# Two later places on a DMA queue: an encoder's attention bias tables, and the turning of an FFN's last gated half

## The chip, the cores and the metric

The kernel runs on one core of a Trainium2 chip. The metric is the device time of one execution in microseconds; lower is better. A program of this kind is one instruction stream per engine (TensorE, VectorE, ScalarE, GpSimd and SyncE), and the engines meet only at semaphores. In the profile they are PE (with PEld for its weight loads), DVE, ACT, POOL and SP. "SPq" and "POOLq" are the queues in which SyncE and GpSimd issue DMA transfers.

## The reference

The model is an encoder trunk with two layers over 512 tokens of width 1024, all in float32. What matters of it:

```python
def swiglu(x, w_in, w_out):
    g, u = jnp.split(x @ w_in, 2, axis=-1)          # 1024 -> 2 x 2816
    return (jax.nn.silu(g) * u) @ w_out             # 2816 -> 1024

def mixer(h, w_in, gate_bias, rpb, w_na_out, w_f_out, w_o):
    z = h @ w_in                                    # q, k, v, uf, ga, gf
    ...
    y_na = neighbourhood_attention(q, k, v, rpb) @ w_na_out
    y_f = fourier_mix(uf) @ w_f_out
    g_na = jax.nn.sigmoid(ga + gate_bias[0])
    g_f = jax.nn.sigmoid(gf + gate_bias[1])
    return (g_na * y_na + g_f * y_f) @ w_o

for l in range(2):
    x = x + 0.5 * swiglu(rms_norm(x, ffn1_norm[l]), ffn1_w_in[l], ffn1_w_out[l])
    x = x + mixer(rms_norm(x, mix_norm[l]), ...)
    x = x + 0.5 * swiglu(rms_norm(x, ffn2_norm[l]), ffn2_w_in[l], ffn2_w_out[l])
out = rms_norm(x, final_norm)
```

The attention adds a learned bias per head (from `rpb`) to its scores before the softmax. There are eight heads, and the kernel reads the bias as one expanded table of 384 KB per head.

## The kernel before

**Numbers.** Every float32 operand is split into a high and a low part, and each product is three matmuls (high x high, low x high, high x low; lines 508, 509 and 511). A granule of weights, 128 x 1024, is loaded by DMA into a buffer `raw`, ScalarE copies its high part (`whi`, three buffers), and VectorE subtracts to get the low part (`wlo`). The class `Stream` does this in a fixed order of granules: it loads 8 granules ahead (`FETCH`) and prepares 2 ahead (`AHEAD`) of the one that TensorE uses. Some granules are sums of two matrices. For these a second, accumulating load comes from POOL's queue, or VectorE adds two buffers (L164).

**Strassen.** Most products are one step of a Strassen-like scheme with seven products for a 2 x 2 block. Hence the names A, B, C, the product numbers 1 to 7, and the sums and differences of operands on VectorE.

**An FFN** (`stage_ffn`, four times) has an input half and an output half. The input half runs over blocks `jb` of 512 hidden features. Each block ends with two gated halves, one for each half of the tokens: `z2` (tokens 256 to 511, j = 1) after product 3, and `z1` (j = 0) after product 4. Each must be turned, so that features lie on partitions: `apart` copies the 16-bit words apart on ScalarE (`zs`, two copies, L346), SP issues a DMA transpose (`zt`, L347), and later `joined` copies the words together on ScalarE into a tile `at` (L356). The helper `halves` does the first two and puts the result on the list `turned`; `joined` takes the next from that list.

The output half is a list of 21 steps (product, chunk of rows): steps 0 to 2 are product 1, 3 to 5 product 2, then products 5, 6, 7, 3 for each of three chunks (6 to 17), and 18 to 20 product 4. `make(i)` forms the high and low part of step i's operand (names `c1h`, `c1l`, `c2h` and so on, after the product) up to two steps ahead. The last block's `z1` is read first by step 5, and its `z2` by the sum for step 15. Their joins are placed in the step loop:

```python
            if i == 3:
                turned.reverse()
                joined()
            if i == 5:
                joined()
```

**The mixer** (`stage_mixer`, twice) starts with products of the projection (`proj_UV`), with single projections of q and k between them. Its weight buffers come from a shared pool of slots. The bias tables (`bm`, four buffers) lie in the mixer's own pool, which is opened in the last steps of the FFN ahead, over the space of that FFN's weight buffers. `bias_for(hp)` loads the tables of two heads on SP's queue, and `Probs.maxes` (L1297) is their first reader.

**Order.** A scheduler orders each engine's instructions from the program's order and its own estimates of time. It may move an instruction ahead of others on its engine, DMA issues on SP included. `tc.keep_in_program_order(ins)` pins one instruction to its place, `tc.issue_after(ins)` puts what its block issues on the engine of `ins` behind `ins`, and `manual_schedule` keeps whole engines in program order for a block.

Of the kernel before, what the change touches and what calls it, by code (L numbers as in the profile page):

```python
# [13 lines left out]
U16 = mybir.dt.uint16  # L14
AF = mybir.ActivationFunctionType
# [3 lines left out]
P = 128  # L19
# [8 lines left out]
NH, DH = 8, 64  # L28
# [62 lines left out]
def encoder_kernel(  # L91
    ctx: ExitStack, tc: tile.TileContext, xin, xtr, wst, gains, gfin, gbias, bias_in, dft, chan, ident_in, rot, out
):
    nc = tc.nc
# [16 lines left out]
    def slot(dt=F32, s="k", shape=(4, 256)):  # L111
        return kp.tile([P, *shape], dt, tag="k", name=nm(s), bufs=23)
# [39 lines left out]
    class Item:  # L152
# [26 lines left out]
        def prep(self, nxt):  # L179
            n = self.raw.n  # L180
            hi = wp.tile([P, 1024], F32R, tag="whi", name=nm("whi"), bufs=3)[:, 0:n]
            lo = wp.tile([P, 1024], F32R, tag="wlo", name=nm("wlo"), bufs=3)[:, 0:n]
            t = self.raw.t
            self.summed()
            if self.neg:
                S.activation(hi, t, AF.Copy, scale=-1.0)  # L186
                self.last = V.scalar_tensor_tensor(lo, t, -1.0, hi.bitcast(F32), ALU.mult, ALU.subtract)  # L187
            else:
                for c in range(0, n, n // self.parts):
                    cs = slice(c, c + n // self.parts)  # L190
                    S.activation(hi[:, cs], t[:, cs], AF.Copy)  # L191
                    if nxt:
                        nxt.summed()
                    self.last = V.tensor_tensor(lo[:, cs], t[:, cs], hi[:, cs].bitcast(F32), ALU.subtract)  # L194
            if self.then:
                G.dma_start(out=t, in_=wst[GRAN_AT[self.then]][:, 0:n], accum_op=ALU.add)
            self.out = (hi, lo)
# [113 lines left out]
    ws = Stream()  # L311
# [26 lines left out]
            V.scalar_tensor_tensor(r, t, 1.5, r, ALU.add, ALU.mult)  # L338
        return r

    def apart(z):

        s, t = slot(U16, "zs", (2, 4, 2, P)), slot(U16, "zt", (2, 4, 256))
        words = z.bitcast(U16).rearrange("p b (q f h) -> p h q b f", q=4, h=2)
        for h in range(2):
            S.activation(s[:, h], words[:, h], AF.Copy)  # L346
        nc.sync.dma_start_transpose(  # L347
            out=t.rearrange("p h q (b t) -> p (h q b) t", b=2), in_=s.rearrange("p h q b f -> p (h q b f)")
        )
        return t  # L350

    def joined_words(to, t):

# [261 lines left out]
    def stage_ffn(norm, nxt, late):  # L615
# [75 lines left out]
        late_at, turned = [], []  # L691

        def halves(z, j, f0):

            turned.append((apart(z), j, f0))
# [26 lines left out]
        def settle_at():  # L722
            while late_at:
                to_at(*late_at.pop(0))
# [47 lines left out]
        def make(i):  # L772
            if i < len(steps) and i not in made:
                m, c, f = steps[i]
                made[i] = hl(f(), c, f"c{m}")
# [95 lines left out]
        for jb in range(0 if first else 1, NB):  # L871
            f0 = 2 + 4 * jb
            if first and jb == 0:
                with tc.manual_schedule(engines={mybir.EngineType.DVE, mybir.EngineType.Activation}):
                    pa = pair("A")
                    product(pa, acts[1], K4, True)
                    for j in range(2):
                        t = snap(pcl[j])
                        pcl[j] = [t[:, 0, :], t[:, 1, :]]
                    s1 = snap(pa)  # L880
                    second(s1)
                    pb = pair("B")
                    product(pb, acts[5], K4, True)
                    sb = snap(pb)
                    norm.rstd()
            else:
                pa, pb, s1, sb = two(jb)
                settle_at()
            product(pa, acts[6], K4, False, again=True)
            s2 = snap(pa)  # L890
            settle_at()
            if turned:
                joined()
            if jb or not first:
                second(s1)
            else:
                plain_out()
            z1 = gate(s1, 0)
            product(pa, acts[7], K4, False, again=True)
            if turned:  # L900
                joined()
            less(pa, sb)
            product(pb, acts[3], K4, False, again=True)
            less(pb, s2)
            if jb == NB - 1:
                make(0)
                make(1)
            z2 = gate(s2, 1)
            times(z2, [sb[:, 0, :], sb[:, 1, :]], 1)
            halves(z2, 1, f0)  # L910
            if jb == NB - 1:
                make(2)
            product(pa, acts[4], K4, False, again=True)
            times(z1, pa, 0)
            halves(z1, 0, f0)
# [4 lines left out]
        for i, (m, c, _) in enumerate(steps):  # L920
# [13 lines left out]
            )  # L934
            if i == 0:
                settle_at()
            if i == 3:
                turned.reverse()
                joined()
            if i == 5:  # L940
                joined()
            if m == 4 and c == 0 and not late:
                with tc.manual_schedule(engines={mybir.EngineType.DVE, mybir.EngineType.Activation}):
# [101 lines left out]
    def stage_mixer(l, norm, nxt):  # L1045
# [75 lines left out]
        def proj_UV():  # L1121

            acts, combine = combos(norm, None)
            ws.depth = 8
            steps = {m: combine(m) for m in (5, 6, 7, 4)}

            def step(m, n=1):
                for _ in range(n):
                    next(steps[m])

            step(5)
            def t1():
                step(5, 2)
                norm.squares(1, 0)

            pa = pair("A")
            product(pa, acts[1], K4, True, hook=t1)
            root = norm.rstd_steps()
            next(root)
            ws.items[ws.prepped + 1].summed()  # L1140
            next(root)
            norm.spread(R)
            ws.prep(ws.pos + 3)
            low10 = norm.quad_high(*norm.due.pop(0))
            s1 = snap(pa)
            norm.low01()
            step(6, 2)
            pb = pair("B")
            product(pb, acts[5], K4, True, hook=low10)
            sb = snap(pb)  # L1150
            S.activation(small("sq", 1), ones, AF.Exp)
            step(6)
            q0 = proj_T(DH**-0.5)
            step(7)
            product(pa, acts[6], K4, False, again=True, hook=lambda: step(7))
            s2 = snap(pa)
            k0 = proj_T(None)
            step(7)
            step(4, 2)
            q0 = q0()  # L1160
            step(4)
            pc = pair("C")
            product(pc, acts[2], K4, True)
            q[0] = q0()
            q1 = proj_T(DH**-0.5)
            k0 = k0()
            less(pc, s1)
            k[0] = k0()
            product(pb, acts[3], K4, False, again=True)
            q1 = q1()  # L1170
            less(pb, s2)
            uh, ul = slot(F32R, "uh", (2, T)), slot(F32R, "ul", (2, T))
            S.activation(uh, s2, AF.Copy)
            q[1] = q1()
            norm.flip()
            V.tensor_tensor(ul, s2, uh.bitcast(F32), ALU.subtract)
            S.activation(mir, mirror, AF.Copy)
            flipped = []

            def turn():  # L1180
                for c in range(2):
                    pm = bank()
                    PE.matmul(pm, mir, uh[:, 1 - c, :], start=True, stop=False)
                    PE.matmul(pm, mir, ul[:, 1 - c, :], start=False, stop=True)
                    t = tmp(s="uf")
                    S.activation(t, pm, AF.Copy, scale=norm.rflip[:, c : c + 1])
                    flipped.append(t)


            k1 = proj_T(None, hook=turn)  # L1190
            constants()
            us, ue = [[], []], []
            for c in range(2):
                for op in (ALU.add, ALU.subtract):
                    w = tmp(s="ue")
                    V.scalar_tensor_tensor(w, s1[:, c, :], norm.r[:, c : c + 1], flipped[c], ALU.mult, op)
                    ue.append(high_of(w, "u"))
                    us[c].append(None)
            for i, low_of in enumerate(ue):
                us[i // 2][i % 2] = low_of()  # L1200
            product(pa, acts[7], K4, False, again=True, ahead=0)
            ws.depth = FETCH
            return us, k1, pa, sb, acts[4]
# [55 lines left out]

        o, q, k, bms = [], {}, {}, {}  # L1260

        def bias_for(hp):
            bms[hp] = []
            for e in range(2):
                res = mp.tile([P, 3, 256], F32, tag="bm", name=nm("bm"), bufs=4)
                nc.sync.dma_start(out=res, in_=bias_in[(l * NH + 2 * hp + e)])
                bms[hp].append(res)

        def att_scores(i):
# [227 lines left out]
        with tc.manual_schedule(engines={mybir.EngineType.DVE, mybir.EngineType.Activation}):  # L1497
            with tc.manual_schedule(engines={mybir.EngineType.PE}):
                u, k1, pa, sb, acts4 = proj_UV()
                fp = [four_pos(0), four_pos(1)]  # L1500
                bias_for(0)
                k1 = k1()
                ws.prep(ws.pos + 2)
                bt = [rotated(fp[0])]
# [485 lines left out]
```

## Time and profile before

| | us |
|---|---|
| median of 3 runs | 1855.29 (1852.73 to 1857.38) |
| profiled execution | 1856.45 |
| its span, first to last instruction | 1854.7 |
| PE busy | 1841.4 (99%) |
| DVE busy | 1605.3 (87%) |
| ACT busy | 1311.6 (71%) |
| POOL busy | 171.5 (9%) |

The profile is of one execution. Its rows give a start, a duration and, in brackets, the idle time of that engine just before and what ended it. Matmuls overlap in TensorE, and their ends are modelled, so their pace is read from start to start. In a table of waits a row has the waiting engine, what released it, the time in total, the number of times and the longest. A row with "xN" stands for N instructions in a row. For a DMA issue the duration is that of the issue, not of the transfer.

### The profile page before, as it was taken

The numbers are of one execution on the slowest core, as the hardware profiler recorded it, in microseconds if no ns is written. First come the engines' busy times: TensorE is split into PE (matmuls) and PEld (weight loads), VectorE is DVE, ScalarE is ACT, GpSimd is POOL, SyncE is SP. The second block draws the span as 40 slices with busy tenths as digits, with TensorE's granted clock in tenths as the row PEclk, the third lists the DMA queues.
The fourth block names the chain that finished last, engine by engine and source line by source line (L and its number), as shares of the span: only waits on it lengthen the run. The fifth ranks groups of instructions, "written<-read, shape, count | busy, mean of one in ns | idle before, by whom it ended". The sixth has DMA issues, their size and how long they took to land.

```text
span 1854.7 us, 24607 instructions
## 1 busy us (share of the span) xinstructions
PE 1841.4 (99%) x8862; PEld 1530.4 (83%) x8862; DVE 1605.3 (87%) x1950; ACT 1311.6 (71%) x1780; POOL 171.5 (9%) x210
## 2 busy tenths in 40 slices
PE   9999999999999999999999999999999999999997
PEld 7888888888888888888788888888888888888886
DVE  7878899786989987889998888997869899887898
ACT  6777875668676777777666777766676776777865
POOL 0001010100111100001010100101001101000010
PEclk9999999999999999999999999999999999999999
DMA  9898798933886788879888887988249867889794
GB/s 302 227 231 218 197 272 271 226 97 105 251 230 174 183 219 226 210 201 269 243 197 222 225 219 196 271 281 205 70 154 235 226 174 182 233 206 217 220 285 133
DMA packets 198458, 394.21 MB, mean 213 GB/s; under 512 B 103808, under 2 KB 103936, under 8 KB 198336
## 3 DMA queue, kind: packets, MB, share of 16 engines
q1 hardware_dynamic: 169664, 294.30, 49.3%
q0 software_dynamic: 28528, 98.33, 29.6%
q8 instruction: 69, 1.13, 0.3%
q14 instruction: 53, 0.43, 0.1%
q10 hardware_dynamic: 144, 0.02, 0.0%
HBM read 365.85 MB, written 2.11 MB: 198 GB/s over the span
## 4 chain that ended last, share of the span: by engine, by line
PE 92%; DVE 4%; DMA 2%; issue 1%; ACT 1%; SPq 0%; DVEq 0%; POOL 0%; ACTq 0%; POOLq 0%
PE A L508 10%; PE A L511 10%; PE A L509 10%; PE o L511 6%; PE o L508 6%; PE o L509 6%; PE B L509 5%; PE B L508 5%; PE B L511 5%; PE ps L315 4%; PE ps L316 3%; PE ps L317 3%; PE C L508 3%; PE C L509 3%; PE C L511 3%
## 5 line engine op out<-in xcount | busy, mean ns | idle before, releaser
L194 DVE TENSOR_TENSOR wlo<-raw,whi 128x1024 fp32r<-128x1024 f32 (+1 forms) x534 | 631.5, 1192 | 172.0 <-ACT whi L191 171.3
L191 ACT ACTIVATE whi<-raw 128x1024 fp32r<-128x1024 f32 (+1 forms) x534 | 546.0, 1033 | 255.9 <-DVE raw L164 61.2
L150 POOL DMA_DIRECT2D raw<-in_wst_dram x166 | 144.3, 891 | 1341.8 <-DMA raw<-in_wst_dram 754.2
L164 DVE TENSOR_TENSOR raw<-raw,raw 128x1024 f32<-128x1024 f32 (+1 forms) x150 | 178.8, 1193 | 2.0
L509 PE MATMUL A<-whi,xl 128*128 128x512 f32 x400 | 155.7, 389 | 0.0
L508 PE MATMUL A<-whi,xh 128*128 128x512 f32 x400 | 155.7, 389 | 0.0
L356 ACT ACTIVATE at<-zt 128x1024 uint16<-128x1024 uint16 (+2 forms) x96 | 110.4, 1168 | 19.0 <-DMA zt<-zs 19.0
L186 ACT ACTIVATE whi<-raw 128x1024 fp32r<-128x1024 f32 (+1 forms) x83 | 86.0, 1036 | 47.0 <-issue 12.5
L511 PE MATMUL A<-wlo,xh 128*128 128x512 f32 x400 | 115.0, 389 | 0.0
L187 DVE SCALAR_TENSOR_TENSOR wlo<-raw,whi 128x1024 fp32r<-128x1024 f32 (+1 forms) x83 | 98.4, 1194 | 11.3 <-ACT whi L186 11.3
L511 PEld LDWEIGHTS A<-wlo,xh 128*128 128x128 f32 x400 | 75.1, 188 | 15.6
L508 PEld LDWEIGHTS A<-whi,xh 128*128 128x128 f32 x400 | 75.1, 188 | 15.4
L509 PEld LDWEIGHTS A<-whi,xl 128*128 128x128 f32 x400 | 75.1, 188 | 15.4
L508 PE MATMUL C<-whi,xh 128*128 128x512 f32 x208 | 81.1, 390 | 0.3 <-ACT whi L191 0.3
L509 PE MATMUL C<-whi,xl 128*128 128x512 f32 x208 | 81.0, 389 | 0.0
L509 PE MATMUL B<-whi,xl 128*128 128x512 f32 x208 | 81.0, 389 | 0.0
L508 PE MATMUL B<-whi,xh 128*128 128x512 f32 x208 | 80.9, 389 | 0.0
L346 ACT ACTIVATE zs<-th 128x1024 uint16<-128x1024 uint16 x80 | 79.4, 1041 | 0.9 <-DVE th L737 0.9
L730 ACT ACTIVATE th<-sn,rh 128x512 f32<-128x512 f32 x80 | 55.1, 716 | 34.0 <-DVE sn L583 33.1
L578 ACT ACTIVATE sn<-A 128x512 f32<-128x512 f32 x104 | 59.0, 584 | 24.8 <-PE A L511 24.8
L511 PE MATMUL C<-wlo,xh 128*128 128x512 f32 x208 | 59.8, 389 | 0.0
L511 PE MATMUL B<-wlo,xh 128*128 128x512 f32 x208 | 59.8, 389 | 0.0
(438 smaller groups left out, 4680.2 us busy)
## 6 DMA issues: line engine op xcount, KB each, us to landing
raw<-in_wst_dram SPq DMA_DIRECT2D x470, 512.0 KB, 5.8
raw<-in_wst_dram POOLq DMA_DIRECT2D x174, 512.0 KB, 7.9
raw<-in_wst_dram SPq DMA_DIRECT2D x30, 256.0 KB, 4.2
bm<-in_bias_dram SPq DMA_DIRECT2D x16, 384.0 KB, 3.6
x<-in_xin_dram SPq DMA_DIRECT2D x4, 512.0 KB, 10.2
raw<-in_wst_dram POOLq DMA_DIRECT2D x8, 256.0 KB, 9.3
dft<-in_dft_dram POOLq DMA_DIRECT2D x8, 256.0 KB, 4.3
gb<-in_gbias_dram SPq DMA_DIRECT2D x4, 512.0 KB, 15.1
```

Source lines behind the costliest of these rows:

```text
L150: G.dma_start(out=self.t, in_=wst[GRAN_AT[self.plus]][:, 0 : self.n], accum_op=ALU.add)
L164: V.tensor_tensor(self.raw.t, self.raw.t, self.add.t, ALU.add)
L186: S.activation(hi, t, AF.Copy, scale=-1.0)
L187: self.last = V.scalar_tensor_tensor(lo, t, -1.0, hi.bitcast(F32), ALU.mult, ALU.subtract)
L191: S.activation(hi[:, cs], t[:, cs], AF.Copy)
L194: self.last = V.tensor_tensor(lo[:, cs], t[:, cs], hi[:, cs].bitcast(F32), ALU.subtract)
L315: PE.matmul(ps, lh, rh, start=start, stop=False, skip_group_check=again)
L346: S.activation(s[:, h], words[:, h], AF.Copy)
L356: S.activation(to[:, w], t[:, w], AF.Copy)
L508: PE.matmul(ps, lh, rh, start=start, stop=False, skip_group_check=again)
L509: PE.matmul(ps, ll, rh, start=False, stop=False, skip_group_check=again)
L511: PE.matmul(ps, lh, rl, start=False, stop=stop, skip_group_check=again)
```

## The change

It has two parts.

In the mixer, the first call of `bias_for` moves from behind the projection (where `four_pos` has run) to an earlier place in the program, after the third product of the projection, and its two loads are pinned to that place in SP's order.

In an FFN's last block, `z2` is still copied apart where it was, but its DMA transpose is issued only after step 1 of the output half, pinned to that place. So `z1`, turned at the end of the block, is on the list first. The join of `z1` stays at step 3 and is placed on ScalarE behind the high part of the last weights that have been prepared; the join of `z2` moves from step 5 to step 7. To this end `apart` is divided into `words_apart` and `turned_words`, and the weights' preparation keeps its ScalarE instruction as `first`.

```diff
@@ Item.prep
-                S.activation(hi, t, AF.Copy, scale=-1.0)
+                self.first = S.activation(hi, t, AF.Copy, scale=-1.0)
...
-                    S.activation(hi[:, cs], t[:, cs], AF.Copy)
+                    self.first = S.activation(hi[:, cs], t[:, cs], AF.Copy)
@@
-    def apart(z):
-
-        s, t = slot(U16, "zs", (2, 4, 2, P)), slot(U16, "zt", (2, 4, 256))
+    def words_apart(z):
+
+        s = slot(U16, "zs", (2, 4, 2, P))
         words = z.bitcast(U16).rearrange("p b (q f h) -> p h q b f", q=4, h=2)
         for h in range(2):
             S.activation(s[:, h], words[:, h], AF.Copy)
-        nc.sync.dma_start_transpose(
+        return s
+
+    def turned_words(s):
+
+        t = slot(U16, "zt", (2, 4, 256))
+        return t, nc.sync.dma_start_transpose(
             out=t.rearrange("p h q (b t) -> p (h q b) t", b=2), in_=s.rearrange("p h q b f -> p (h q b f)")
         )
-        return t
+
+    def apart(z):
+
+        return turned_words(words_apart(z))[0]
@@ stage_ffn, the last block
-            halves(z2, 1, f0)
             if jb == NB - 1:
+                z2 = words_apart(z2)
                 make(2)
+            else:
+                halves(z2, 1, f0)
@@ stage_ffn, the steps of the output half
+            if i == 1:
+                t, ins = turned_words(z2)
+                tc.keep_in_program_order(ins)
+                turned.append((t, 1, f0))
             if i == 3:
-                turned.reverse()
-                joined()
-            if i == 5:
+                with tc.issue_after(ws.items[ws.prepped - 1].first.ins):
+                    joined()
+            if i == 7:
                 joined()
@@ stage_mixer, proj_UV
             s2 = snap(pa)
+            bias_for(0, True)
             k0 = proj_T(None)
@@
-        def bias_for(hp):
+        def bias_for(hp, pinned=False):
             bms[hp] = []
             for e in range(2):
                 res = mp.tile([P, 3, 256], F32, tag="bm", name=nm("bm"), bufs=4)
-                nc.sync.dma_start(out=res, in_=bias_in[(l * NH + 2 * hp + e)])
+                ins = nc.sync.dma_start(out=res, in_=bias_in[(l * NH + 2 * hp + e)])
+                if pinned:
+                    tc.keep_in_program_order(ins)
                 bms[hp].append(res)
@@
                 fp = [four_pos(0), four_pos(1)]
-                bias_for(0)
                 k1 = k1()
```

## The prediction, made before the changed kernel was run

> **What bounds the kernel now.** I read the head of the page first, then the table of what TensorE waited for, then its matmuls in order of time.
>
> ```profile
> span 1854.7 us, 24607 instructions
> PE 1841.4 (99%) x8862; PEld 1530.4 (83%) x8862; DVE 1605.3 (87%) x1950; ACT 1311.6 (71%) x1780; POOL 171.5 (9%) x210
> ...
> PE o L511 <- DVE wlo L194: 1.3, 2, 0.7
> PE ps L136 <- DVE ones L132: 1.2, 1, 1.2
> PE C L508 <- ACT whi L191: 0.3, 1, 0.3
> PE cl L509 <- DVE xl L325: 0.3, 1, 0.3
> PE wC L509 <- DVE m2l L322: 0.2, 1, 0.2
> ...
> 235.36 0.39 PE L508 MATMUL o<-whi,c2h 128*128 128x512 f32 x1
> ...
> 244.88 0.39 PE L508 MATMUL o<-whi,c2h 128*128 128x512 f32 x1
> 245.11 0.39 PE L509 MATMUL o<-whi,c2l 128*128 128x512 f32 x1
> ```
>
> The reader is to see an engine that almost never stops: all waits that the table lists add to 3.3 us. Between 235.36 and 244.88 lie two steps of the output half of an FFN (a first chunk with three row tiles, 18 matmuls, and a second with four, 24): 9.52 us / 42 = 0.2267 us from start to start, though one matmul is shown as 0.39. Small delays hide in that overlap, so I compare equal stretches instead. The output half of an FFN, step loop from its first to its last matmul, runs four times (start and end, length, then busy time and count of PE, PEld, DVE, ACT, POOL, granted clock, DMA share, GB/s):
>
> ```profile
> 220.40:327.86 107.46, 107.46 (x487) 89.22 (x486) 104.32 (x108) 76.72 (x97) 12.63 (x15) 1.00 0.94 263
> 818.36:928.60 110.24, 109.50 (x487) 88.47 (x486) 106.39 (x110) 77.24 (x98) 12.96 (x15) 1.00 0.89 249
> 1140.16:1248.40 108.24, 108.13 (x488) 88.95 (x487) 104.23 (x108) 76.89 (x97) 12.53 (x15) 1.00 0.93 262
> 1739.20:1844.92 105.72, 105.06 (x463) 86.45 (x461) 103.18 (x118) 70.73 (x84) 10.41 (x12) 1.00 0.77 216
> ...
> 315.21 1.91 PE L413 MATMUL tr<-ident,x 128*128 128x128 f32 x16
> ```
>
> The first three have 462 matmuls and 24 transposes; the last has no transposes. Sixteen transposes last 1.91 us with the end of the last one, so 24 are worth some 2.6 us, and the last stretch compares with 107.46 - 2.6 = 104.86. Against the best of them (the first) the others lose 2.78, 0.78 and 0.86 us: 4.4 us in all. That is the whole stock from which the FFN part of the change can gain, 0.24% of the time. The second thing to see is VectorE: 104.32 of 107.46 us busy, 97%. In this stage it has 3 us of slack, so an idle microsecond of VectorE early in it can come back as a stall of TensorE. I take 0.3% of the median, 5.6 us, as about what a measurement of this kernel can tell from no change.
>
> **The bias tables (twice, once a layer).** The change moves two 384 KB loads on SP's queue and nothing else: from an early place, chosen without a fixed order, to behind the weight loads that the program has issued by then.
>
> ```profile
> SPq L1266 <- DVE wlo L194: 13.6, 1, 13.6
> ...
> 321.81 0.80 SPq L1266 DMA_DIRECT2D bm<-in_bias_dram  x2
> 322.66 0.90 SPq L148 DMA_DIRECT2D raw<-in_wst_dram  x2
> 323.60 0.91 SPq L1266 DMA_DIRECT2D bm<-in_bias_dram  x2
> 324.61 3.77 SPq L148 DMA_DIRECT2D raw<-in_wst_dram  x4
> ...
> L1297 DVE CUSTOM_DVE_ANT_0 s<-ps,bm x64: 402/419/425, 395.7 to 1371.4; 128x256 f32<-128x256 f32 x64
> ...
> DMA to landing us min/median/max: 2.8/3.6/8.4
> ```
>
> SP's queue stands 13.6 us at the first table, until VectorE has left the old weight buffers, and six weight loads stand behind it. What that wait costs today is nothing: the table of TensorE's waits names no weights of the mixer's first products, so removing it gains 0. What the new place can cost: by my count the tables come after those six loads, so near 328.4 (324.61 + 3.77), and land by 328.4 + 8.4 = 336.8 at the slowest. Their first reader, the row maxima, starts at 395.7, 59 us later. So 0 on this side too. If the queue should stand still at one of those six loads for 59 us more, the first scores would wait; no row of the queue near there has such a wait. The second pair (323.60) isn't pinned. It can now be the one that comes first and waits the 13.6 us; then this part does nothing at all. ScalarE, POOL and VectorE see no instruction more or less. Value 0, ends -0.5 and +0.5 us (the size of the smaller waits in TensorE's table).
>
> **The FFN's last block (four times).** Nothing is added: four copies that split words and four that join them on ScalarE, and two DMA transposes on SP, stay. Three things move.
>
> First, the transpose of the second token half (j = 1) goes behind that of the first half, to after step 1. On SP's queue:
>
> ```profile
> 223.48 4.54 SPq L347 DMA_TRANSPOSE zt<-zs  x1
> 228.11 1.01 SPq L148 DMA_DIRECT2D raw<-in_wst_dram  x2
> 229.48 3.69 SPq L347 DMA_TRANSPOSE zt<-zs  x1
> 233.26 2.82 SPq L148 DMA_DIRECT2D raw<-in_wst_dram  x3
> ...
> raw<-in_wst_dram SPq DMA_DIRECT2D x470, 512.0 KB, 5.8
> raw<-in_wst_dram POOLq DMA_DIRECT2D x174, 512.0 KB, 7.9
> ```
>
> Two weight loads come up to 4.5 us earlier; those behind the new place come up to 4.5 us later. Loads are issued eight granules ahead, each worth 12 matmuls x 0.2267 = 2.72 us, so 21.8 us; a load and an accumulating load on top take 5.8 + 7.9 = 13.7. The 8.1 us between them cover a shift of 4.5. Without that cover it would cost up to 4.5 us a time. The first half's transpose keeps its place at 229.48: it waits for its own two copies on ScalarE, so it lands no earlier.
>
> Second, the join of the first half (2 copies, L356) is held on ScalarE behind the last prepared weights, which at that point are the second granule of step 4. Its row of before and the neighbours, in the first FFN and in the second:
>
> ```profile
> 235.11 1.06 ACT L191 ACTIVATE whi<-raw 128x1024 fp32r<-128x1024 f32 x1 [0.98 <-PE o L509]
> 236.08 2.57 ACT L356 ACTIVATE at<-zt 128x1024 uint16<-128x1024 uint16 x2
> 238.51 1.03 ACT L191 ACTIVATE whi<-raw 128x1024 fp32r<-128x1024 f32 x1
> 239.45 1.04 ACT L321 ACTIVATE c2h<-at 128x1024 fp32r<-128x1024 f32 x1
> ...
> 237.58 1.22 DVE L194 TENSOR_TENSOR wlo<-raw,whi 128x1024 fp32r<-128x1024 f32 x1
> 239.57 1.23 DVE L194 TENSOR_TENSOR wlo<-raw,whi 128x1024 fp32r<-128x1024 f32 x1 [0.78 <-ACT whi L191]
> 240.72 1.22 DVE L322 TENSOR_TENSOR c2l<-at,c2h 128x1024 fp32r<-128x1024 f32 x1
> ...
> 833.86 2.58 ACT L356 ACTIVATE at<-zt 128x1024 uint16<-128x1024 uint16 x2 [3.30 <-DMA zt<-zs]
> 836.31 1.03 ACT L191 ACTIVATE whi<-raw 128x1024 fp32r<-128x1024 f32 x1
> ...
> 837.38 1.23 DVE L194 TENSOR_TENSOR wlo<-raw,whi 128x1024 fp32r<-128x1024 f32 x1 [1.76 <-ACT whi L191]
> ...
> 1160.54 1.23 DVE L194 TENSOR_TENSOR wlo<-raw,whi 128x1024 fp32r<-128x1024 f32 x1 [1.99 <-ACT whi L191]
> ...
> 1758.38 1.22 DVE L194 TENSOR_TENSOR wlo<-raw,whi 128x1024 fp32r<-128x1024 f32 x1 [0.79 <-ACT whi L191]
> ```
>
> First FFN. The weights copy at 238.51 would now come first. It reuses the buffer (one of three) of step 3's first granule, whose last reader is the eighth matmul: 235.36 + 7 x 0.2267 + 0.39 = 237.3. So copy 237.3 to 238.4, join to 240.8, the operand's high part (c2h) to 241.8, its low part on VectorE to 243.0. TensorE needs it at 245.11: 2.1 us to spare, where before it had 245.11 - 240.72 - 1.22 = 3.2. No direct stall. Queued behind the held join on ScalarE are c2h and the weights of step 5, on VectorE the low parts that follow. VectorE: its wait of 0.78 goes, but after the second weights (ready at 238.4, done 237.58 + 1.14 x 2 = 239.9) it now waits for c2h until 241.8: 1.9 us instead of 0.78, so about 1.1 worse. The third FFN shows what that is worth: with 1.99 idle at the same place its stretch is 0.78 us longer than the first one's. I take +0.8 for the first FFN, and the same for the fourth (0.79 idle now). The third is already in that state: 0. In the second FFN the 3.30 us wait for the transpose goes, as the weights at 836.31 no longer stand behind it; but VectorE is no further at the end of this passage: now it does both weights' low parts and c2l from 837.38 on, three operations of 1.15 (239.57 to 240.72), to 840.8; by the working of the first FFN, which lies 818.36 - 220.40 = 597.96 earlier, c2l as the last of the three would end at 243.0 + 597.96 = 841.0. The gain is only in the earlier release of a weight buffer. That FFN loses 2.0 us more than the third with the same idle there; I take a third of it, -0.6.
>
> Third, the join of the second half goes from step 5 to step 7, 2.6 us of ScalarE's time. Its reader is the sum for step 15, far behind; ScalarE is 71% busy in this stretch (76.72 of 107.46). Taken at 0; without the cover, up to 2.6 us.
>
> **Sum.** 0.8 - 0.6 + 0 + 0.8 + 0 = +1.0 us. The profiled execution took 1856.45 us, of which its span is 1854.7 and 1.75 lie around it; it is 1.16 above the median of 1855.29. By the profile 1857.4; moved to the median, 1856.3. The bounds: -4.4 if all four stretches become as good as the best, and +6.7 (the slower rival).
>
> **The rivals.** *Slower: VectorE can't make it up.* The held join costs VectorE 1.9 us or more in each FFN, the late second join takes ScalarE from the weights at step 7, and accumulating loads then run late as in the second FFN. The price, if all four become as bad as the worst stretch shown: 2.78 + 0 + (2.78 - 0.78) + (2.78 - 0.86) = 6.7 us, 1862.0. Place: the weights' low parts in steps 7 to 17. It decides when VectorE's idle time in a stretch passes the 3 us of slack. For it: 97% busy. Against it: 1.1 us of new idle in two of four.
>
> *The waits go and all of the loss with them:* -4.4, 1850.9. For it: the 3.30 us row and the 1.76 behind it are just what the pin attacks. Against it: c2h itself moves behind the weights. It stays within 0.3%.
>
> *It doesn't do what it says:* the second pair of tables takes the first one's wait, and transposes and joins fall where other waits hide them: 1855.3.
>
> *TensorE's matmul time isn't the bound:* if weights loads set the pace and matmuls only stretched over waits that the change shortens, the four stretches could fall to their PEld time: 431.7 - 353.1 = 78.6 us less, 1776.7. Against it: 42 matmuls at an even 0.2267 us in a stretch where nothing is waited for. The Trainium skill, "Perfetto Trace Analysis", section "Identifying the Most-Contended Engine", says that matmul busy time is a poor measure of how near a kernel is to its limit and that LDWEIGHTS busy time should be taken. By that rule the 83% would leave much room; the even starts speak for a full engine.
>
> **How the numbers follow.** Forecast (a net of -2 to +3 us, no change that can be told) 0.50; no effect 0.15; all of the loss gone 0.15; the slower rival, from 5 us up, 0.17, of which 0.01 stays below 5.6 us; the matmul rival 0.01; 0.02 for a gain over 5.6 us from places that the profile doesn't show as waits. Faster by over 0.3%: 0.03. Slower by over 0.3%: 0.16. Within: 0.81. Predicted 1856.3. The range goes from 1850.9 to 1861.5, into the lower part of the slower case.
>
> **What would show it.** Right: the four stretches at about 108.3, 109.6, 108.2 and 106.5 us; no wait of L356 for its transpose in the output halves; a weights copy ahead of L356 in each; VectorE's wait before c2l near 2 us; the first bias load with no 13.6 us before it, or that wait passed on to the second pair. Wrong: a stretch over 111 us, TensorE waiting for c2l or for weights in steps 5 to 9, or a mixer whose first products wait.

## The result and the profile after

The changed kernel takes 1858.26 us (median of 16 runs, 1856.83 to 1862.26), the kernel before 1855.42 beside it (16 runs, 1852.73 to 1857.64). The ratio is 1.0014, 95% interval [1.0008, 1.0021]: slower by some 2.6 us. The interval doesn't hold 1, so the difference is real, but it is less than the 0.3% that I had named as the bound. The profiled execution took 1858.61 us, its span is 1856.8, 2.1 above the span of before.

The head of its page, and rows of the table of what TensorE waited for (total, times, longest). L511 and L509 of before are now L519 and L517:

```profile
span 1856.8 us, 24633 instructions
PE 1841.3 (99%) x8862; PEld 1529.3 (82%) x8862; DVE 1605.3 (86%) x1950; ACT 1310.7 (71%) x1780; POOL 171.0 (9%) x210
...
PE o L519 <- DVE wlo L194: 1.4, 2, 0.7
PE ps L136 <- DVE ones L132: 1.2, 1, 1.2
PE A L516 <- ACT sn L586: 0.7, 1, 0.7
PE cl L516 <- ACT whi L191: 0.6, 1, 0.6
PE ps L316 <- DVE xl L426: 0.4, 2, 0.2
```

All busy times are the same within 1.1 us. The last three of these rows are not in the table of before, nor are two more of 0.3 us. Rows for `A L516` and `cl L516` also stand in profiles of kernels without a loss (0.2 and 0.8 us in e7 below). `ps L316 <- DVE xl` comes twice, in the first projection of each mixer; of the fourteen profiles of this document just those eight have it whose mixers start late. The four output halves (start and end, length, busy times and counts, clock, DMA share, GB/s):

```profile
220.37:327.88 107.51, 107.51 (x487) 89.09 (x486) 104.03 (x108) 75.53 (x93) 12.48 (x15) 1.00 0.94 274
818.96:927.55 108.59, 107.93 (x487) 89.01 (x486) 105.37 (x109) 76.61 (x97) 12.80 (x15) 1.00 0.90 252
1139.13:1247.49 108.36, 108.29 (x488) 88.80 (x487) 104.05 (x108) 75.47 (x93) 12.60 (x15) 1.00 0.93 272
1739.91:1847.11 107.20, 106.11 (x463) 86.04 (x461) 103.19 (x118) 70.45 (x84) 10.35 (x12) 1.00 0.76 213
```

Against before they are +0.05, -1.65, +0.12 and +1.48 us: together nothing. So the loss isn't where the FFN part works, or the single profile hides it; the runs below look at both. On SP's queue the bias tables stand where they were expected, without a wait, and their first reader comes 68 us later:

```profile
300.28 28.13 SPq L148 DMA_DIRECT2D raw<-in_wst_dram  x15
328.46 0.90 SPq L1281 DMA_DIRECT2D bm<-in_bias_dram  x2
339.41 0.33 SPq L148 DMA_DIRECT2D raw<-in_wst_dram  x1
339.79 0.91 SPq L1281 DMA_DIRECT2D bm<-in_bias_dram  x2
...
L1314 DVE CUSTOM_DVE_ANT_0 s<-ps,bm x64: 400/418/425, 396.5 to 1371.2; 128x256 f32<-128x256 f32 x64
```

The held join in the first FFN, on ScalarE and VectorE in order of time (idle time before, and what ended it, in brackets):

```profile
237.42 1.07 ACT L191 ACTIVATE whi<-raw 128x1024 fp32r<-128x1024 f32 x1 [1.25 <-PE o L517]
238.39 2.57 ACT L364 ACTIVATE at<-zt 128x1024 uint16<-128x1024 uint16 x2
240.82 1.03 ACT L191 ACTIVATE whi<-raw 128x1024 fp32r<-128x1024 f32 x1
241.75 1.04 ACT L321 ACTIVATE c2h<-at 128x1024 fp32r<-128x1024 f32 x1
...
237.54 2.34 DVE L194 TENSOR_TENSOR wlo<-raw,whi 128x1024 fp32r<-128x1024 f32 x2
241.88 1.23 DVE L194 TENSOR_TENSOR wlo<-raw,whi 128x1024 fp32r<-128x1024 f32 x1 [2.00 <-ACT whi L191]
243.03 1.22 DVE L322 TENSOR_TENSOR c2l<-at,c2h 128x1024 fp32r<-128x1024 f32 x1
```

VectorE now idles 2.00 us there, as worked out (1.9), yet this stretch is within 0.05 us of before. On SP's queue the first half's transpose, which comes first now, has not kept its place:

```profile
226.94 1.86 SPq L352 DMA_TRANSPOSE zt<-zs  x1
228.89 1.03 SPq L148 DMA_DIRECT2D raw<-in_wst_dram  x1
229.97 4.04 SPq L352 DMA_TRANSPOSE zt<-zs  x1
```

It is issued at 226.94 instead of 229.48, because ScalarE's two copies for it start 2.5 us earlier (224.93 instead of 227.46), with fewer weights copies ahead of them.

### The profile page after: what moved, and what is told of

It is laid out like the page before. It is cut to its first block, busy times and chain, and to the rows that moved or that the text cites. A ratio compares the mean times of both kernels' runs of the same rounds, so it can differ in the third digit from the quotient of the medians.

```text
span 1856.8 us, 24633 instructions
## 1 busy us (share of the span) xinstructions
PE 1841.3 (99%) x8862; PEld 1529.3 (82%) x8862; DVE 1605.3 (86%) x1950; ACT 1310.7 (71%) x1780; POOL 171.0 (9%) x210
## 4 chain that ended last, share of the span: by engine, by line
PE 85%; DVE 6%; DMA 4%; issue 3%; ACT 2%; POOL 0%; SPq 0%; DVEq 0%; ACTq 0%; POOLq 0%
PE A L516 9%; PE A L517 9%; PE A L519 9%; PE o L519 5%; PE o L517 5%; PE o L516 5%; PE B L516 5%; PE B L517 5%; PE B L519 5%; PE ps L315 3%; PE ps L316 3%; PE ps L317 3%; DMA raw<-in_wst_dram 3%; PE C L517 2%; PE C L516 2%
## 5 line engine op out<-in xcount | busy, mean ns | idle before, releaser
L517 PE MATMUL A<-whi,xl 128*128 128x512 f32 x400 | 155.7, 389 | 0.0
L516 PE MATMUL A<-whi,xh 128*128 128x512 f32 x400 | 155.7, 389 | 0.0
L364 ACT ACTIVATE at<-zt 128x1024 uint16<-128x1024 uint16 (+2 forms) x96 | 111.0, 1168 | 12.5 <-DMA zt<-zs 12.5
L519 PE MATMUL A<-wlo,xh 128*128 128x512 f32 x400 | 115.1, 389 | 0.0
L519 PEld LDWEIGHTS A<-wlo,xh 128*128 128x128 f32 x400 | 75.1, 188 | 15.6
L517 PEld LDWEIGHTS A<-whi,xl 128*128 128x128 f32 x400 | 75.1, 188 | 15.5
L516 PEld LDWEIGHTS A<-whi,xh 128*128 128x128 f32 x400 | 75.1, 188 | 15.4
L517 PE MATMUL C<-whi,xl 128*128 128x512 f32 x208 | 81.0, 389 | 0.0
L517 PE MATMUL B<-whi,xl 128*128 128x512 f32 x208 | 81.0, 389 | 0.0
L516 PE MATMUL C<-whi,xh 128*128 128x512 f32 x208 | 80.9, 389 | 0.0
L516 PE MATMUL B<-whi,xh 128*128 128x512 f32 x208 | 80.9, 389 | 0.0
L519 PE MATMUL B<-wlo,xh 128*128 128x512 f32 x208 | 59.8, 389 | 0.0
L519 PE MATMUL C<-wlo,xh 128*128 128x512 f32 x208 | 59.8, 389 | 0.0
```

Source lines behind the costliest of these rows:

```text
L364: S.activation(to[:, w], t[:, w], AF.Copy)
L516: PE.matmul(ps, lh, rh, start=start, stop=False, skip_group_check=again)
L517: PE.matmul(ps, ll, rh, start=False, stop=False, skip_group_check=again)
L519: PE.matmul(ps, lh, rl, start=False, stop=stop, skip_group_check=again)
```

## Where the time went

I looked for the first place where the same matmul starts later than in the kernel before and stays late. It is the mixer's start. The matmuls of TensorE in the kernel before and then in the changed one, first those that end the first FFN, then the mixer's first projection, then the end of the mixer's product 6 (start, duration):

```profile
327.41 0.61 PE L511 MATMUL o<-wlo,c4h 128*128 128x512 f32 x2
339.65 0.39 PE L315 MATMUL ps<-xh,whi 128*128 128x512 f32 x1
339.88 0.39 PE L316 MATMUL ps<-xl,whi 128*128 128x512 f32 x1
350.08 0.62 PE L511 MATMUL A<-wlo,t6h 128*128 128x512 f32 x2
```

```profile
327.43 0.61 PE L519 MATMUL o<-wlo,c4h 128*128 128x512 f32 x2
339.67 0.39 PE L315 MATMUL ps<-xh,whi 128*128 128x512 f32 x1
340.29 0.50 PE L316 MATMUL ps<-xl,whi 128*128 128x512 f32 x1 [0.22 <-DVE xl L426]
350.85 0.61 PE L519 MATMUL A<-wlo,t6h 128*128 128x512 f32 x2
```

22.67 us before, 23.42 after: 0.75 us, though the table of waits owns up to 0.2. VectorE shows why. Before, then after:

```profile
287.47 1.22 DVE L750 TENSOR_TENSOR at<-at,at 128x1024 f32<-128x1024 f32 x1
...
315.42 1.22 DVE L322 TENSOR_TENSOR c4l<-at,c4h 128x1024 fp32r<-128x1024 f32 x1
...
325.66 1.23 DVE L187 SCALAR_TENSOR_TENSOR wlo<-raw,whi 128x1024 fp32r<-128x1024 f32 x1 [1.17 <-ACT whi L186]
326.81 1.22 DVE L418 TENSOR_TENSOR xl<-xr,xh 128x1024 fp32r<-128x1024 f32 x1
327.94 1.28 DVE L756 SCALAR_TENSOR_TENSOR x<-o,x 128x512 f32<-128x512 f32 x2
...
338.05 1.22 DVE L418 TENSOR_TENSOR xl<-xr,xh 128x1024 fp32r<-128x1024 f32 x1
```

```profile
313.12 2.47 DVE L764 SCALAR_TENSOR_TENSOR x<-o,x 128x512 f32<-128x512 f32 x4
315.52 1.21 DVE L758 TENSOR_TENSOR at<-at,at 128x1024 f32<-128x1024 f32 x1
...
318.92 1.21 DVE L322 TENSOR_TENSOR c4l<-at,c4h 128x1024 fp32r<-128x1024 f32 x1
...
326.74 0.68 DVE L764 SCALAR_TENSOR_TENSOR x<-o,x 128x512 f32<-128x512 f32 x1
328.09 0.69 DVE L764 SCALAR_TENSOR_TENSOR x<-o,x 128x512 f32<-128x512 f32 x1 [0.66 <-PE o L519]
328.69 1.22 DVE L426 TENSOR_TENSOR xl<-xr,xh 128x1024 fp32r<-128x1024 f32 x1
...
339.01 1.22 DVE L426 TENSOR_TENSOR xl<-xr,xh 128x1024 fp32r<-128x1024 f32 x1
```

The edit moved a join at step 3 and one at step 5. At step 20, some 70 us later, the scheduler has put the sum for the last operand (`at<-at`) behind four updates of x (315.52); before, the last sum of this half started at 287.47. The last `c4l` comes 3.5 us later, the work behind it shifts, and in the end the mixer's first `xl` stands behind two updates of x, the second of which waits for the FFN's last matmul. Before, it stood ahead of them: 328.69 instead of 326.81. At the next `xl` 0.96 us of that is left (339.01 against 338.05), and TensorE waits for it. Most of the delay is still there when the second output half begins: from the matmul at 327.64 to the first of that half it is 490.72 us before (818.36 - 327.64) and 491.30 after (818.96 - 327.66).

## The experiments

Each of these kernels ran in five rounds beside the kernel before. Diffs are against the changed kernel unless another is named. All but e2 have the bias tables in their new place. In the table "turned late" says whether the second half's transpose comes after step 1, "held" whether the first join is placed behind the last prepared weights, and "second join" gives its step; "start" is the time from the FFN's last matmul to a fixed later one in the first and in the second mixer (22.44 in the kernel before: from 327.64, the second of its row at 327.41, to 350.08); "second" and "last" are the lengths of the output halves, one profile each.

| kernel | turned late | held | second join | ratio to before, 95% | start | second | last |
|---|---|---|---|---|---|---|---|
| before | no | no | 5 | 1 | 22.44, 26.97 | 110.24 | 105.72 |
| e1 tables only | no | no | 5 | 0.9998 [0.9989, 1.0006] | 22.44, 26.97 | 109.53 | 105.15 |
| changed | yes | yes | 7 | 1.0014 [1.0008, 1.0021] | 23.19, 27.75 | 108.59 | 107.20 |
| e2 FFN part only | yes | yes | 7 | 1.0012 [1.0002, 1.0022] | 23.19, 27.77 | 109.06 | 106.81 |
| e3 | yes | yes | 5 | 1.0041 [1.0029, 1.0053] | 23.19, 27.73 | 108.56 | 109.30 |
| e4 | yes | no | 7 | 1.0005 [0.9997, 1.0014] | 23.19, 27.77 | 107.82 | 107.31 |
| e5 sum first | yes | yes | 7 | 1.0011 [1.0003, 1.0020] | 22.44, 26.97 | 108.42 | 107.45 |
| e6 | no | no | 7 | 1.0033 [1.0020, 1.0045] | 23.19, 27.73 | 109.22 | 108.66 |
| e7 | yes | no | 5 | 0.9992 [0.9983, 1.0001] | 22.44, 26.97 | 107.40 | 108.35 |
| e8 | no | yes | 7 | 1.0017 [1.0008, 1.0026] | 23.19, 27.72 | 109.19 | 106.35 |
| e9 | in the first three | no | 5 | 0.9988 [0.9979, 0.9997] | 22.44, 26.97 | 107.40 | 106.67 |
| e10 | first three: as changed | | | 1.0006 [0.9997, 1.0015] | 23.19, 27.76 | 108.82 | 104.87 |
| e11 | no | yes | 5 | 1.0013 [1.0004, 1.0022] | 23.19, 27.73 | 107.61 | 109.73 |
| e12 | in the last | no | 5 | 1.0002 [0.9993, 1.0011] | 22.44, 26.97 | 107.88 | 105.79 |

**Each part alone (e1, e2).** e1 is the kernel before with the `bias_for` lines of the change, e2 the change without them.

> Only the mixer's part of the change: the first bias tables pinned behind the weights, the FFNs as before. Theory A (all of the loss comes from the FFN part, through the order of ScalarE and VectorE; the tables are free): the time of before, 1855.4 us, within 1 us, with the 13.6 us wait of SP's queue gone or passed on and TensorE's start of the mixer at an unchanged distance from the end of the FFN. Theory B (the six weight loads that now start some 13 us earlier disturb the end of the FFN or the mixer's first products): +1.3 us or more, of which about 0.7 us shows in each layer in the 20 us after the mixer's first matmul.

> Only the FFN part of the change: the bias tables where they were. Theory A: the same loss as the whole change, 1858.2 us (+2.8), with the mixers' first products late by 0.7 us each although the tables are as before, the second FFN's output half about 1.7 us shorter and the last one's about 1.4 us longer. Theory B: half of the loss or less, +0.5 to +1.4, and no delay in the mixers' first products.

Measured 1855.57 us and 1858.09. The tables are free as far as the interval tells (0.9989 to 1.0006), and the FFN part alone has as much of a loss as the whole change.

**The second join back at step 5 (e3), and the hold taken out (e4).**

```diff
-            if i == 7:
+            if i == 5:
                 joined()
```
```diff
             if i == 3:
-                with tc.issue_after(ws.items[ws.prepped - 1].first.ins):
-                    joined()
+                joined()
```

> The whole change, but the second half's join stays at step 5 instead of step 7. If the late join is what costs (it takes 2.6 us of ScalarE at a place where VectorE waits on ScalarE's weights): about 1 to 1.5 us faster than the change, 1857, most of it in the last FFN. If the held first join is what costs: no difference, 1858.2.

> The whole change, but the first half's join isn't held behind the weights. If the hold is what costs (1.1 us of new VectorE idle time in the first and fourth FFN): 1 to 2 us faster than the change, 1856.5 to 1857, and ScalarE's wait for the transpose in the second FFN is back at about 3 us. If it is free: no difference, 1858.2.

Measured 1864.19 and 1857.66. Of the two times expected of e3 neither came. Step 7 isn't the fault: with the late turn and the hold, step 5 is clearly worse, and in its profile the third and the last output half carry most of it (109.20 and 109.30 us, against 108.36 and 107.20). Taking the hold out (e4) changes less than these intervals can tell. The sign named for the hold didn't come: no output half of e4 has ScalarE waiting for a transpose. The late turn removes that wait by itself, as the earlier issue at 226.94 suggests; none of the kernels has it in an FFN that turns late.

**The step-20 sum put back (e5).** The updates of x after step 17 are issued behind the sum, which is traced ahead of them; `summed` keeps what `comb` issues:

```diff
             elif m == 3:
-                update(ps[1], 0, 1, -1)
-                update(ps[3], 0, 1, 1)
+                if late:
+                    update(ps[1], 0, 1, -1)
+                    update(ps[3], 0, 1, 1)
+                else:
+                    make(i + 3)
+                    with tc.issue_after(summed[-1].ins):
+                        update(ps[1], 0, 1, -1)
+                        update(ps[3], 0, 1, 1)
```

> All of the change, and in every FFN but the last the difference for the last output product's third operand (at<-at, step 20) is traced ahead of the two updates of x after step 17, which are queued behind it on VectorE. Nothing is left out. Theory A (the displaced step-20 operand starts the mixers late): the sum stands ahead of the updates again as in the kernel before, the third c4h comes near 91.5 us after the first output product and not at 96.9, the mixer's first products start 0.75 us earlier in each layer, and the time is 1.5 us under the changed kernel: 1856.7. Rival B (the mixers start late because SP's queue or the weights are late, and the operand's place is only a symptom): the mixers start as late as in the changed kernel and the time stays at 1858.2.

```profile
313.50 1.22 DVE L760 TENSOR_TENSOR at<-at,at 128x1024 f32<-128x1024 f32 x1
...
327.69 1.22 DVE L426 TENSOR_TENSOR xl<-xr,xh 128x1024 fp32r<-128x1024 f32 x1
328.82 1.28 DVE L766 SCALAR_TENSOR_TENSOR x<-o,x 128x512 f32<-128x512 f32 x2
...
328.24 0.61 PE L519 MATMUL o<-wlo,c4h 128*128 128x512 f32 x2
350.91 0.62 PE L519 MATMUL A<-wlo,t6h 128*128 128x512 f32 x2
```

VectorE's rows and TensorE's of e5: `xl` stands ahead of the updates again, and 350.91 - 328.24 = 22.67, as before. So the sum's place is what delays the mixers, as theory A says, and not rival B's queue or weights. The price is not regained: the time is 1858.03. The updates now run later, and from the first `c4h` product to the last matmul the first three FFNs take 16.95, 16.96 and 16.92 us instead of the 16.52, 16.53 and 16.51 of the changed kernel: 1.27 us. Of the 1.5 us that leaves 0.2, which the intervals of 1.0011 and 1.0014 can't tell apart. The order that the scheduler chose here was about as good as the one that I pinned.

**The three moves one by one (e6, e7, e8, e11).** e6 and e8 turn the second half early, and e6 is free of the hold as well; e7 is the late turn alone; e11 is the hold alone. The edits are those of e3 and e4 and, for an early turn:

```diff
-                z2 = words_apart(z2)
+                halves(z2, 1, f0)
...
-            if i == 1:
-                t, ins = turned_words(z2)
-                tc.keep_in_program_order(ins)
-                turned.append((t, 1, f0))
             if i == 3:
+                turned.reverse()
```

> The change without the late turn and without the hold: the transposes stand where they stood before, the first join is free at step 3, and only the second join is moved, from step 5 to step 7 (the bias tables at their new place). Theory A (moving a join later is by itself what pushes the step-20 operand behind the updates of x): mixers late by 0.75 us each as in the changed kernel, the last output half up to 1.6 longer, the second FFN's 1 to 1.6 shorter; 1856.5 to 1858. Rival B (the late turn does it): the mixers start as before, 1855.5, or 1854.5 if step 7 also helps the second FFN.

> The change with the late turn of the second half alone: no hold, second join at step 5 as before (bias tables at their new place). Theory A: the operand of step 20 stays where it was and the mixers start as before; but the join at step 5 now has to wait for a transpose issued some 15 us later, so that VectorE or ScalarE stands before c6 and c7 in each FFN: 1857 to 1864, by up to 2 us an FFN, and the output halves carry all of it. Rival B (the late turn costs nothing, and the 1864 with a hold and step 5 came from the hold): 1855.5.

> The change without the late turn: the second half's transpose is issued where it was before, the first join is held behind the weights copy at step 3, the second join stands at step 7 (bias tables at their new place). Theory A (the joins' places, not the transposes, are what costs): as the changed kernel, 1858.0, with mixers late by 0.75 us each. Rival B (the late turn costs): 1855.5 to 1856.5, with mixers on time.

> The hold of the first join alone: both transposes early, the second join at step 5 as before (bias tables at their new place). Theory F (the hold pushes the first join against the second, so that both fall before c6 and c7 and VectorE comes late in every FFN): 1860 to 1864, like the hold with the late turn and step 5 (1864.2). Rival G (the hold hurts only where the second half is turned late): 1855.5 to 1857.

Measured 1861.62, 1854.34, 1859.26 and 1858.14. What the table then says is plain in one column: the mixers start 0.75 us late with the hold or with step 7, in every such kernel but e5, and never with the late turn alone. In the first layer the delay stays: from the same matmul up to the first matmul of the second output half the six kernels with the early start take 490.70 to 490.94 us, the eight others 491.28 to 492.30. In the second layer the same two ranges overlap (491.03 to 491.69 and 491.28 to 493.65). The times go the same way: 0.9988 to 1.0002 with the early start, but for e5, and 1.0005 to 1.0041 with the late one. For e6 the late mixers are as theory A had them, but its time lies above both forecasts. For e7 the rival was right and theory A wrong: with step 5 the late turn costs nothing. The second transpose comes 6.5 us later there, not the 15 that I had assumed (9.60 against 3.08 us after the first product of the first output half). Nor are the effects sums of parts. The hold costs 0.13% alone and 0.49% on top of the late turn with step 5 (0.9992 to 1.0041), but if anything gains where the second join stands at step 7 and the turn is early (1.0033 to 1.0017). e11 lies between its theories F and G; in its profile the mixers start late and the last output half, at 109.73 us, is the longest of all.

**One FFN or another (e9, e10, e12).** e9 has the late turn in the first three FFNs, e12 in the last alone, and e10 the whole change in the first three. `late` is true in the last FFN; for e9, without the hold and with step 5 as above:

```diff
             if jb == NB - 1:
-                z2 = words_apart(z2)
+                if late:
+                    halves(z2, 1, f0)
+                else:
+                    z2 = words_apart(z2)
...
-            if i == 1:
+            if i == 1 and not late:
```

> The late turn of the second half in the first three FFNs only, without the hold and with the second join at step 5; the last FFN as in the kernel before (bias tables at their new place). Theory D (the late turn is worth 1 to 3 us in the second and third FFN, and costs 2 us in the last, where it bunches the weight loads on SP's queue and an accumulating load comes late): the last output half's excess over its own computing falls from 3.6 to under 1 us, the time is 1852.5, faster than both kernels by 0.2 per cent. Rival E (the differences of 1 to 2 us between the output halves are chance of the single profile): 1854.3 as with the late turn in all four FFNs, or 1855.5.

> The whole change in the first three FFNs, the last FFN as in the kernel before. Theory D: the 1.6 us that the changed kernel loses in the last output half come back, 1856.4; what is left over the kernel before is the mixers' later start, 1.5, against the second FFN's gain. Rival E: 1858.0 as the changed kernel.

> The late turn in the last FFN only, without the hold and with step 5; the first three FFNs as in the kernel before (bias tables at their new place). Theory D: the last output half has an excess of 2 to 3.6 us over its own computing, with ScalarE waiting for an accumulating load near 47 us after the half's first product; 1857.5. Rival E: 1855.5 and an excess near 1 us.

Measured 1854.31, 1857.36 and 1855.64. In turn the last output half of e10 (order as before), the second and the last of e12, the second of e1 and the last of e7. The second of e12 and of e1 have the order of before, and the last of e12 and of e7 have one order:

```profile
1739.90:1844.77 104.87, 104.87 (x463) 86.45 (x461) 103.08 (x118) 70.72 (x84) 10.33 (x12) 1.00 0.78 218
```
```profile
818.21:926.09 107.88, 107.88 (x487) 89.11 (x486) 106.31 (x110) 77.56 (x98) 12.96 (x15) 1.00 0.92 254
...
1736.39:1842.18 105.79, 105.05 (x463) 86.28 (x461) 103.16 (x118) 70.53 (x84) 10.36 (x12) 1.00 0.77 216
```
```profile
817.99:927.52 109.53, 108.80 (x487) 88.71 (x486) 106.36 (x110) 77.27 (x98) 12.96 (x15) 1.00 0.90 250
```
```profile
1736.68:1845.03 108.35, 107.02 (x463) 85.76 (x461) 103.24 (x118) 70.28 (x84) 10.32 (x12) 1.00 0.75 211
```

For e9 and e12 rival E has the better of it; e10, at 1.0006, is where theory D put it (1856.4 against 1855.4 is 1.0005), but its interval holds rival E's 1.0014 too. With one and the same order of instructions, the second output half took 110.24, 109.53 and 107.88 us (before, e1, e12), and the last took 108.35 and 105.79 (e7, e12). A difference of 1 to 2 us in one stretch of one profile is no evidence; I had built theory D on such differences, and e12 refutes its part on the last FFN. What is left for the last FFN is a comparison of groups. As in the kernel before (before, e1, e9, e10) it took 105.72, 105.15, 106.67 and 104.87, mean 105.60; as in the changed kernel (changed, e2, e5) 107.20, 106.81 and 107.45, mean 107.15. The means are 1.55 us apart. The groups don't overlap, but 106.67 and 106.81 are only 0.14 apart and one order alone spread by 2.6 us, so this is a hint and no proof. The times agree with it: e10 is 0.0008 below the changed kernel, 1.5 us, though the two intervals meet.

e9 is the version that beats both kernels: 0.9988, 0.12% below before. Its interval ends at 0.9997, and it is the best of twelve, so a part of the 0.12% may be chance. Why the late turn helps isn't shown. What it changes at its place is the same in every profile: the first half's transpose is issued 6.57 us after the first product of the output half, without it 9.07 (9.39 once). The second output half is at 107.40 in both kernels that have the late turn there without the hold and with step 5 (e7, e9), below all three of the order before, but that is again five profiles.

## Why the prediction was right or wrong

The time, 1858.26, lies in the range, the case (slower, but within 0.3%) and the direction were the forecast. The size wasn't: +1.0 was forecast for the medians, some +2.6 to +2.8 came, and most of the terms of the sum were not what the runs show. That the time was met is partly luck: the range is 10.6 us wide, and a term of 1.5 us was not in the sum at all. The 5.6 us that I took as what a measurement can tell was too coarse as well; the interval of the result reaches 0.0007 either way, some 1.2 us.

- **Bias tables, 0:** right, down to the place (328.46, forecast 328.4) and the wait that goes. e1 shows it alone. The slowest table took 14.5 us to land, not 8.4, which is still far ahead of its reader.
- **Transpose of the second half, 0:** right as a bound on its harm; e7 has it alone at 0.9992. The step that the first half's transpose keeps its place and lands no earlier was wrong: in every FFN that turns late it is issued 2.5 us earlier.
- **Hold in the first FFN, +0.8:** the mechanics were right. `c2h` started at 241.75, where I had it ending at 241.8, because one more weights copy stood ahead of it; VectorE idled 2.00 us. The price was wrong: with the change the first output half took 107.51, 107.41 and 107.43 us (changed, e2, e10), without it 107.46, 107.62 and 107.51 (before, e1, e12). With the hold alone (e11) the first three halves took 107.41, 107.61 and 107.40. So 1.2 us more of VectorE's idle time cost nothing in a stretch where it is 97% busy. The longest first halves, 109.5 and 109.0, are those of e4 and e6, which have step 7 without the hold. I had priced it by the third FFN's length, whose excess over the first can't be told from chance: it took 107.40 in e1 and e12.
- **Second FFN, -0.6:** can't be told from 0. With the change 108.59, 109.06 and 108.82; without it 110.24, 109.53 and 107.88. The profile of before had shown the longest of the three.
- **Third FFN, 0:** near that, 108.36, 107.79 and 107.64 against 108.24, 107.40 and 107.40: +0.25 by the means, which can't be told from 0 either.
- **Fourth FFN, +0.8:** mis-sized if the groups hold, +1.55. The late second join, which I had at 0, belongs to the same stretch; which of the three moves it is isn't settled: the late turn alone gave 108.35 and 105.79.
- **The mixers:** the missing term, and the step that failed. I followed the moved instructions to step 7 and not to step 20. "A mixer whose first products wait" stood among the signs that the prediction was wrong, and it did: 2 x 0.75 = 1.5 us.

With these, 0 + 0 + 0 + 0 + 0.25 + 1.55 + 1.5 = 3.3 us against 2.6 to 2.8. The difference is within what the groups leave open. Of the terms only the mixers' start is shown by an experiment, as a delay in the profile (e5); the last FFN's is argued.

Of the signs that it was right, most came: no L364 waits for its transpose in any output half (before, 3.3 us in the second and 1.1 in the third), a weights copy stands ahead of it, and VectorE's wait there is 1.91 to 2.00 us in all four. The stretches took 107.51, 108.59, 108.36 and 107.20 us where about 108.3, 109.6, 108.2 and 106.5 were named. Of the signs that it was wrong, no stretch is over 111 us and no wait of TensorE that the table lists lies in steps 5 to 9; the mixers' wait came. The slower rival (VectorE can't make it up in every FFN) isn't what the change does, but e3 comes near it: 1864.19, with three of its halves 0.35 to 3.6 us longer than before. The matmul rival fell: no kernel here has a median below 1854, and its price was 78.6 us. The last output half of e10 has no idle TensorE at all (104.87 busy of 104.87), and with nothing to wait for it still takes 104.87 us, 462 matmuls at 0.227, and not its PEld time of 86.45. The Trainium skill, "Perfetto Trace Analysis", section "Identifying the Most-Contended Engine", names two measures in place of matmul busy time, MFU (matmul work over the peak) and the busy share of the weight loads, and the prediction took the second alone. By that share this stretch would have 18% of room; the measurement decides for the matmuls.

**What stays open:** why the second join at step 7 costs 0.33% with an early turn and 0.13%, with intervals that meet, with a late one; why the hold costs so much with a late turn and step 5; which move lengthens the last output half, if any does; and what the late turn gains. The orders that the scheduler writes differ in many places between these kernels, and no run here takes them apart one by one.

## What to carry to other kernels

Where a scheduler writes the order, an edit's price isn't at the edit: compare the order of every engine to the end of the next stage, above all what stands ahead of the first operands of the following stage. Look for a matmul that starts late and stays late, and not for waits: the table showed 0.2 us where 0.75 were lost. And before a stretch of one profile becomes a term of a sum, ask how much the same stretch varies with the same code; here it was 2.4 us, as much as the whole effect, while the mixer's start took one of two values in all fourteen profiles, each to within 0.05 us.

## What was not expected of the hardware

The same order of ScalarE and VectorE instructions gave a second output half of 107.88 to 110.24 us, at DMA shares of 0.92 to 0.89, while the mixer's start repeated to 0.01 us. Accumulating loads by themselves don't explain it: the stretch from there to the third output half, with 19 of them, took 211.79 us in twelve of the fourteen profiles and at most 212.01. What makes the second output half vary isn't shown.
